# The head of each MLP: pinned norm matmuls, earlier first weights, three square buffers, and k outermost

## The chip, the cores and the metric

The kernel runs on one core of a Trainium2 chip. Its engines are TensorE (PE: matmuls and, listed apart as PEld, its weight loads), VectorE (DVE), ScalarE (ACT), GpSimd (POOL) and SyncE (SP, which here only issues DMAs). Each takes its own instructions in the order written; semaphores tie them together. The metric is the device time of one execution in microseconds.

## The reference

A two-layer bidirectional encoder is applied to a prompt of 256 and a sample of 512 tokens with shared weights (model width 1024, 64 per head, MLP width 4096). Cut to what matters here:

```python
for layer in range(2):
    h = rmsnorm(x, ln_mix[layer])
    x = x + attention(h) @ w_out          # layer 0: neighbourhood + grouped-query, layer 1: differential
    h = rmsnorm(x, ln_mlp[layer])         # x * rsqrt(mean(x*x) + 1e-6) * g
    x = x + square(relu(h @ w_up[layer])) @ w_down[layer]
return rmsnorm(x, ln_f)
```

All is float32.

## The kernel before

**Layout.** The 512 and 256 tokens are laid side by side, so x is eight tiles x[0] to x[7] of 128 features by 768 tokens. Every float32 operand of a large matmul is split in two fp32r parts, `hi` (a rounded copy, by ACT) and `lo` (the rest, by DVE), and a product is three matmuls: hi x hi, hi x lo, lo x hi. For weights this is `wsplit` (L77 to L82), with tiles wraw (three buffers, loaded through SP at L75), whi and wlo (four buffers each, `whilo`, L90).

**The head** is `out_proj_norm` (L753) with `up_plain` (L823). The output projection's last two of eight k tiles are applied here, in two token halves of 384 (`EVEN`), since they depend on the last attention heads. For each half: eight products of six matmuls (opc, L778), each added to x[m] by DVE (L780), squared by ACT (L144) and summed into acc (L149), the second to fifth tile's by POOL, the sixth's and seventh's by DVE; the last square stays apart in `parts`. `rstd` (L152) multiplies acc and that last square with ones on TensorE (ss, L158), DVE scales (ms, L161), POOL takes the power -1/2 (rt, L163); `spread` (L166) brings rt to all partitions on TensorE (pb, L177) and DVE copies it to R (L179). Then for each of the eight k, DVE forms xn = x * g * R (L763), ACT its hi part xh (L766) and DVE its lo part xl (L767).

The square's buffer has the tag `sq`, one buffer of 768 columns. xn, `up_plain`'s av and the sums' t share the tag `st`, three buffers of 384 columns.

**The up projection** comes in groups of four blocks (f) of 128 hidden features. In group 0, `up_plain`: for each half, for each f, for each k, three matmuls (upc, L837); then Relu, Square and the hi part hh by ACT (L839 to L842) and the lo part hl by DVE (L843). f 0 and 1 use the first pair of weight tiles, f 2 and 3 the second. The other groups use `up_fast` (L849), a Strassen-like scheme that needs sums of the xn parts: T (three sets of four pairs) and t4. `sums` (L797) forms them after `up_plain`: for each of four kk it recomputes two n = x * g * R over all 768 tokens (L763; tag `av`, three buffers), then t1, t2, t3 and t4 (L805 to L813), with their splits.

**The down projection** of a group (`down`, L922) makes eight output tiles, two at a time, each in two PSUM tiles (dna, dnb, L202), and DVE adds them to x (L932). Group 0's is called with `cover`, which takes the first two of four k for both of the first two tiles ahead of the others. It runs after `sums` in the order written. The last group of layer 1 has `final` (L936), which does the down projection, the sum of squares, the last norm (L964) and the stores for 512 tokens and then for 256; its matmuls are fin (L953).

PSUM has eight banks: three for the tag `mm`, five for `at` (L33).

**What sets the order.** A planner orders each engine's instructions ahead of time: it simulates the program with its own costs, takes of the ready instructions the one written first, and gives out buffers as it goes. Reads and writes of the same tile keep their written order, so a DVE add to x[k] comes after the sums' reading of x[k]. Nothing else fixes where `rstd` and `spread` stand among TensorE's products.

## Time and profile before

| what | value |
|---|---|
| median of 3 runs | 1855.36 us (1855.0 to 1857.76) |
| the profiled execution | 1855.08 us, of which the span of the profile is 1853.3 us |
| mean granted clock of TensorE | 0.986 |
| PE busy, PEld busy | 97%, 92% |
| DVE, ACT, POOL busy | 61%, 45%, 14% |
| layer 0's head, first opc to first dna | 350.88 to 423.56 us |
| layer 1's head, first opc to first dna | 1278.72 to 1354.77 us |

In the rows of the timeline, the first two numbers are start and length in us, then engine, line, operation, `out<-in` by the program's tile names, shapes, and in brackets the engine's idle time before it with what ended it. A row of waits reads "engine tile line <- engine tile line waited for: total us, times, longest". A row of stretches has bounds, length, each engine's busy time with its instructions, TensorE's granted clock, the DMA engines' busy share and GB/s. A row of groups ends with busy us, mean ns of one, and idle us before them.

### The profile page before, as it was taken

The numbers are of one execution on the slowest core, as the hardware profiler recorded it, in microseconds if no ns is written. First come the engines' busy times: TensorE is split into PE (matmuls) and PEld (weight loads), VectorE is DVE, ScalarE is ACT, GpSimd is POOL, SyncE is SP. The second block draws the span as 40 slices with busy tenths as digits, with TensorE's granted clock in tenths as the row PEclk, the third lists the DMA queues.
The fourth block names the chain that finished last, engine by engine and source line by source line (L and its number), as shares of the span: only waits on it lengthen the run. The fifth ranks groups of instructions, "written<-read, shape, count | busy, mean of one in ns | idle before, by whom it ended". The sixth has DMA issues, their size and how long they took to land.

```text
span 1853.3 us, 28804 instructions
## 1 busy us (share of the span) xinstructions
PE 1796.7 (97%) x11382; PEld 1710.5 (92%) x11382; DVE 1123.6 (61%) x2238; ACT 828.7 (45%) x1733; POOL 259.4 (14%) x340
## 2 busy tenths in 40 slices
PE   7999999989999999999999999999899999999997
PEld 7878888889999999999999999987899999999996
DVE  8877555568645544554566676775685455455545
ACT  6765443344533433343435555554445334334434
POOL 4411000110100100010221221211101001000003
PEclk9999999989999999999999999999799999999998
DMA  5111224102523433343410111122025334333432
GB/s 171 47 32 38 72 64 162 52 23 69 134 60 96 114 88 78 95 110 88 133 53 25 45 47 38 35 93 65 24 57 131 75 97 110 85 81 91 114 86 80
DMA packets 52328, 146.33 MB, mean 79 GB/s; under 512 B 6113, under 2 KB 8929, under 8 KB 52193
## 3 DMA queue, kind: packets, MB, share of 16 engines
q1 hardware_dynamic: 38080, 119.82, 20.5%
q0 software_dynamic: 12096, 22.03, 7.6%
q10 hardware_dynamic: 2016, 2.64, 0.4%
q8 instruction: 90, 1.47, 0.3%
q14 instruction: 46, 0.37, 0.1%
HBM read 137.38 MB, written 6.29 MB: 78 GB/s over the span
## 4 chain that ended last, share of the span: by engine, by line
PE 88%; DVE 6%; ACT 3%; POOL 2%; issue 1%; DMA 1%; DVEq 0%; SPq 0%; ACTq 0%; POOLq 0%
PE dna L202 13%; PE dnb L202 13%; PE upx L882 13%; PE dqk L189 8%; PE upz L882 6%; PE dvp L189 4%; PE opa L202 4%; PE upy L882 3%; PE upc L837 3%; PE npa L202 2%; PE ds L268 2%; PE dpv L711 2%; PE opb L202 2%; PE fin L953 2%; PE qp L189 1%; PE vp L189 1%
## 5 line engine op out<-in xcount | busy, mean ns | idle before, releaser
L81 ACT ACTIVATE whi<-wraw 128x1024 fp32r<-128x1024 f32 (+2 forms) x168 | 171.7, 1023 | 194.7 <-PE dnb L202 92.6
L82 DVE TENSOR_TENSOR wlo<-wraw,whi 128x1024 fp32r<-128x1024 f32 (+2 forms) x172 | 201.9, 1180 | 88.8 <-ACT whi L81 87.9
L88 POOL DMA_DIRECT2D wlo<-in_w_up_dram x84 | 74.0, 881 | 847.7 <-ACT wlo L87 462.1
L932 DVE TENSOR_TENSOR x<-dna,x 128x384 f32<-128x384 f32 x120 | 66.7, 556 | 177.1 <-PE dna L202 177.1
L202 PE MATMUL dna<-hh,whi 128*128 128x384 f32 x480 | 162.8, 339 | 3.7 <-DVE x L932 3.7
L202 PE MATMUL dnb<-hh,whi 128*128 128x384 f32 x480 | 162.6, 339 | 0.4 <-DVE x L932 0.4
L202 PE MATMUL dna<-hh,wlo 128*128 128x384 f32 x480 | 162.7, 339 | 0.0
L202 PE MATMUL dna<-hl,whi 128*128 128x384 f32 x480 | 162.4, 338 | 0.0
L202 PE MATMUL dnb<-hh,wlo 128*128 128x384 f32 x480 | 162.4, 338 | 0.0
L202 PE MATMUL dnb<-hl,whi 128*128 128x384 f32 x480 | 162.3, 338 | 0.0
L86 ACT ACTIVATE whi<-wraw 128x512 fp32r<-128x512 f32 x84 | 52.7, 628 | 185.7 <-PE dnb L202 152.6
L189 PE MATMUL dqk<-whi,xh 128*128 128x256 f32 x384 | 115.6, 301 | 0.0
L882 PE MATMUL upx<-T,whi 128*128 128x384 f32 x448 | 115.2, 338 | 0.0
L189 PE MATMUL dqk<-whi,xl 128*128 128x256 f32 x384 | 108.5, 283 | 0.0
L189 PE MATMUL dqk<-wlo,xh 128*128 128x256 f32 x384 | 108.5, 282 | 0.0
L202 PEld LDWEIGHTS dna<-hh,whi 128*128 128x128 f32 x480 | 90.5, 188 | 4.4 <-DVE x L932 4.4
L696 ACT ACTIVATE de<-ds,m 128x512 f32<-128x512 f32 (+1 forms) x96 | 58.4, 613 | 80.4 <-DVE m L694 80.2
L202 PEld LDWEIGHTS dnb<-hh,whi 128*128 128x128 f32 x480 | 90.4, 188 | 0.8 <-DVE x L932 0.8
L202 PEld LDWEIGHTS dna<-hl,whi 128*128 128x128 f32 x480 | 90.5, 188 | 0.0
L202 PEld LDWEIGHTS dna<-hh,wlo 128*128 128x128 f32 x480 | 90.4, 188 | 0.0
L202 PEld LDWEIGHTS dnb<-hl,whi 128*128 128x128 f32 x480 | 90.3, 188 | 0.0
L202 PEld LDWEIGHTS dnb<-hh,wlo 128*128 128x128 f32 x480 | 90.3, 188 | 0.0
(271 smaller groups left out, 5164.4 us busy)
## 6 DMA issues: line engine op xcount, KB each, us to landing
wraw<-in_w_down_dram SPq DMA_DIRECT2D x68, 512.0 KB, 3.9
wraw<-in_w_up_dram SPq DMA_DIRECT2D x64, 512.0 KB, 3.6
wlo<-in_w_up_dram POOLq DMA_DIRECT2D x84, 256.0 KB, 4.9
wraw<-in_w_in_o_dram SPq DMA_DIRECT2D x24, 512.0 KB, 3.6
wraw<-in_w_in_e_dram SPq DMA_DIRECT2D x16, 512.0 KB, 3.7
x<-in_xT_dram SPq DMA_DIRECT2D x16, 384.0 KB, 5.6
nbias<-in_bias_dram SPq DMA_DIRECT2D x20, 256.0 KB, 3.7
wraw<-in_w_out_e_dram SPq DMA_DIRECT2D x8, 384.0 KB, 3.0
```

The source lines that it names most:

```text
L81: nc.scalar.activation(hi, raw, AF.Copy)
L82: nc.vector.tensor_tensor(out=lo, in0=raw, in1=hi.bitcast(F32), op=ALU.subtract)
L86: nc.scalar.activation(hi, raw, AF.Copy)
L88: nc.gpsimd.dma_start(lo, src, accum_op=ALU.add)
L189: nc.tensor.matmul(ps[:, :256], st[:, tk], col(k, part, 0, 256), start=(k == 0 and i == 0), stop=(k == KD - 1 and i == 2))
L202: nc.tensor.matmul(ps[:, : e - s], lhs(k, part), mv[:, s:e], start=(k == 0 and i == 0), stop=(k == nk - 1 and i == 2))
L268: nc.tensor.matmul(out[h], q(a_, hp, qs), k(b_, hp, ks), start=i == 0, stop=i == 2)
L696: nc.scalar.activation(e, s, AF.Exp, bias=m, scale=1.0, accum_out=l2[:, c : c + 1])
L711: nc.tensor.matmul(pv, pt[:, i * P : (i + 1) * P], v[:, k0 // P + i, vc], start=(i == 0), stop=(i == nk - 1))
L837: nc.tensor.matmul(ps, lhs(k, part), mv[:, s:e], start=(n == 0 and j == 0), stop=(n == KD - 1 and j == 2))
L882: nc.tensor.matmul(ps, w[part][:, c], mv, start=(start and kk == 0 and j == 0), stop=(stop and kk == KH - 1 and j == 2), skip_group_check= ...
L932: evac_halves(*ps[mi], lambda p, s: nc.vector.tensor_tensor(out=xm[:, s], in0=p, in1=xm[:, s], op=ALU.add), EVEN)
```

## The change

It has five parts.

1. *Places of the norm matmuls.* `issue_after(i)` binds the instructions traced in its block that run on the engine of i to come after i there. `woven` cuts other products in three pieces: after the first come `rstd`'s matmuls, after the second `spread`'s, then the third. For the first half the pieces are the second half's output products 0 to 2, 3 to 5, and 6 and 7. For the second half they are the up products of the first half: all 48 matmuls of blocks 0 and 1, 24 of blocks 2 and 3, the other 24.
2. *First weights.* The first pair of w_up tiles is loaded and split (`up_ws`) in the text right after the output projection's two tiles, ahead of all products of the head, and passed on.
3. *Square buffers.* The head's squares take the tag `st` with three buffers of 384 columns. `Norm` keeps the start column of each part with it; `final` and the norm ahead of layer 1 keep their one `sq` buffer.
4. *k outermost.* In `up_plain` two blocks go together, one in an `mm` bank, one in an `at` bank: for each k, three matmuls for the one and three for the other, so both end together.
5. *Priorities and banks.* `sums` is traced with its priority lowered by 500 (`LATER`). `final` takes the two PSUM tiles of a pair from `mm` and `at` instead of both from `mm`.

```diff
+LATER = 500
...
     def add(self, x, last=KD):
...
-                sq = self.temp()
-                nc.scalar.activation(sq[:, s], x[:, s], AF.Square)
+                sq = self.temp()[:, : s.stop - s.start]
+                nc.scalar.activation(sq, x[:, s], AF.Square)
...
     def rstd(self):
...
+                    self.last = nc.tensor.matmul(ss[:, 2 * i : 2 * i + 2], part[:, t * P - s0 : (t + 1) * P - s0], ones,
+                                                 start=j == 0, stop=j == len(self.parts) - 1)
...
     def out_proj_norm(src, o, x, g, mp):
         os_ = [split(o[k], "o") for k in (6, 7)]
         ws = [wtile(src, 1024) for _ in range(2)]
+        up_ws = [[wtile("w_up", 1024) for _ in range(2)]]
...
+        norms = [Norm(lambda: mp.tile([P, NH], F32, tag="st", name="sq", bufs=3), half, acc) for half in EVEN]
+        def product(i, m):
+            sl = slice(*EVEN[i])
+            ps = ps_tile(("mm", "at")[m % 2], "opc")[:, :NH]
+            hi, lo = ws[m // 4]
+            for k in range(2):
+                for j, (part, mv) in enumerate(((0, os_[k][0]), (0, os_[k][1]), (1, os_[k][0]))):
+                    c = ((m % 4) * 2 + k) * P
+                    last = nc.tensor.matmul(ps, (hi, lo)[part][:, c : c + P], mv[:, sl],
+                                            start=(k == 0 and j == 0), stop=(k == 1 and j == 2))
+            nc.vector.tensor_tensor(out=x[m][:, sl], in0=ps, in1=x[m][:, sl], op=ALU.add)
+            norms[i].add(x[m], KD - 1)
+            return last
...
-        for i, (s, e) in enumerate(EVEN):
-            sl = slice(s, e)
-            nm = Norm(lambda: mp.tile([P, NT], F32, tag="sq", name="sq", bufs=1), (s, e), acc)
-            for m in range(KD):
...
-            nm.spread(nm.rstd(), R)
+        def split_half(i):
+            sl = slice(*EVEN[i])
             for k in KORD:
...
+        def woven(i, work):
+            nm, last = norms[i], None
+            for step, piece in enumerate(work):
+                with tc.issue_after(last.ins) if last else nullcontext():
+                    last = piece()
+                with tc.issue_after(last.ins):
+                    if step == 0:
+                        rt = nm.rstd()
+                    elif step == 1:
+                        nm.spread(rt, R)
+                        split_half(i)
+                last = nm.last
+        products = lambda i, ms: lambda: [product(i, m) for m in ms][-1]
+        products(0, range(KD))()
+        woven(0, [products(1, ms) for ms in (range(3), range(3, 6), range(6, 8))])
...
-    def up_plain(xs, mp):
-        ws = [[wtile("w_up", 1024) for _ in range(2)] for _ in range(GF // 2)]
+    def up_plain(xs, mp, ws, second_half):
+        ws.append([wtile("w_up", 1024) for _ in range(2)])
...
+        def pair(i, f0):
+            s, e = EVEN[i]
+            pss = [ps_tile(t, "upc")[:, :NH] for t in ("mm", "at")]
+            for n, k in enumerate(KORD):
+                for f, ps in enumerate(pss):
                     for j, (part, mv) in enumerate(((0, xs[k][0]), (0, xs[k][1]), (1, xs[k][0]))):
+                        last = nc.tensor.matmul(ps, lhs(f0 + f, k, part), mv[:, s:e],
+                                                start=(n == 0 and j == 0), stop=(n == KD - 1 and j == 2))
+                if n % 2 and n < KD - 1:
+                    yield last
...
+            yield last
+        first = joined.from_iterable(pair(0, f0) for f0 in range(0, GF, 2))
+        take = lambda n: lambda: [next(first) for _ in range(n)][-1]
+        second_half([take(4), take(2), take(2)])
+        for f0 in range(0, GF, 2):
+            run(pair(1, f0))
         return hs
...
     def final(hs, x, sq):
...
-                ps = [ps_tile("mm", "fin")[:, : e - s] for _ in range(2)]
+                ps = [ps_tile(t, "fin")[:, : e - s] for t in ("mm", "at")]
...
     def mlp(layer, x, state, mp):
-        hs = up_plain(xs, mp)
-        sums()
+        hs = up_plain(xs, mp, up_ws, second_half)
+        with tc.high_priority(offset=-LATER):
+            sums()
         down(hs, x, True)
```

More of the change, by code (lines that the diff above doesn't have):

```diff
@@ L1 @@
 import math
-from contextlib import ExitStack
+from contextlib import ExitStack, nullcontext
+from itertools import chain as joined
 import numpy as np
@@ L135, in __init__ @@
             self.acc = cpool.tile([P, NT], F32, tag="acc", name="acc", bufs=1) if acc is None else acc
-            self.parts = [self.acc]
+            self.parts = [(self.acc, 0)]
         def add(self, x, last=KD):
@@ L142, in add @@
             else:
-                sq = self.temp()
-                nc.scalar.activation(sq[:, s], x[:, s], AF.Square)
+                sq = self.temp()[:, : s.stop - s.start]
+                nc.scalar.activation(sq, x[:, s], AF.Square)
                 if self.n == last:
-                    self.parts.append(sq)
+                    self.parts.append((sq, s.start))
                 else:
                     eng = nc.vector if self.n >= 5 else nc.gpsimd
-                    eng.tensor_tensor(out=self.acc[:, s], in0=self.acc[:, s], in1=sq[:, s], op=ALU.add)
+                    eng.tensor_tensor(out=self.acc[:, s], in0=self.acc[:, s], in1=sq, op=ALU.add)
             self.n += 1
@@ L156, in rstd @@
             for i, t in enumerate(self.tiles):
-                for j, part in enumerate(self.parts):
-                    nc.tensor.matmul(ss[:, 2 * i : 2 * i + 2], part[:, t * P : (t + 1) * P], ones,
-                                     start=j == 0, stop=j == len(self.parts) - 1)
+                for j, (part, s0) in enumerate(self.parts):
+                    self.last = nc.tensor.matmul(ss[:, 2 * i : 2 * i + 2], part[:, t * P - s0 : (t + 1) * P - s0], ones,
+                                                 start=j == 0, stop=j == len(self.parts) - 1)
             ms = spool.tile([P, TT], F32, tag="ms", name="ms", bufs=2)[:, :n]
@@ L176, in spread @@
                     i = self.tiles.index(t)
-                    nc.tensor.matmul(pb[:, t * P - s : t * P - s + P], rt[:, i : i + 1].broadcast_to([P, P]), ident,
-                                     start=True, stop=True)
+                    self.last = nc.tensor.matmul(pb[:, t * P - s : t * P - s + P], rt[:, i : i + 1].broadcast_to([P, P]), ident,
+                                                 start=True, stop=True)
                 nc.vector.tensor_copy(R[:, s:e], pb[:, : e - s])
@@ L757, in out_proj_norm @@
         ws = [wtile(src, 1024) for _ in range(2)]
+        up_ws = [[wtile("w_up", 1024) for _ in range(2)]]
         acc = cpool.tile([P, NT], F32, tag="acc", name="acc", bufs=1)
         R = cpool.tile([P, NT], F32, tag="R", name="R", bufs=1)
-        xs = []
+        xs = [None] * KD
+        norms = [Norm(lambda: mp.tile([P, NH], F32, tag="st", name="sq", bufs=3), half, acc) for half in EVEN]
[11 more added lines that the diff above has]
+            return last
         def normed(k, out, s):
@@ L767, in parts @@
             nc.vector.tensor_tensor(out=lo, in0=src, in1=hi.bitcast(F32), op=ALU.subtract)
-        for i, (s, e) in enumerate(EVEN):
-            sl = slice(s, e)
-            nm = Norm(lambda: mp.tile([P, NT], F32, tag="sq", name="sq", bufs=1), (s, e), acc)
-            for m in range(KD):
-                ps = ps_tile(("mm", "at")[m % 2], "opc")[:, :NH]
-                hi, lo = ws[m // 4]
-                for k in range(2):
-                    for j, (part, mv) in enumerate(((0, os_[k][0]), (0, os_[k][1]), (1, os_[k][0]))):
-                        c = ((m % 4) * 2 + k) * P
-                        nc.tensor.matmul(ps, (hi, lo)[part][:, c : c + P], mv[:, sl],
-                                         start=(k == 0 and j == 0), stop=(k == 1 and j == 2))
-                nc.vector.tensor_tensor(out=x[m][:, sl], in0=ps, in1=x[m][:, sl], op=ALU.add)
-                nm.add(x[m], KD - 1)
-            nm.spread(nm.rstd(), R)
+        def split_half(i):
+            sl = slice(*EVEN[i])
             for k in KORD:
                 if i == 0:
-                    while len(xs) < KD:
-                        xs.append(None)
                     xs[k] = [xpool.tile([P, NT], F32R, tag=t, name=t, bufs=8) for t in ("xh", "xl")]
@@ L818, in last_sum, with lhs @@
                 parts(xs[kk][0][:, b], xs[kk][1][:, b], t4s[kk])
-        return xs, T, sums, last_sum
-    def up_plain(xs, mp):
-        av = []
-        ws = [[wtile("w_up", 1024) for _ in range(2)] for _ in range(GF // 2)]
+        return xs, T, lambda work: woven(1, work), sums, last_sum, up_ws
+    def up_plain(xs, mp, ws, second_half):
+        ws.append([wtile("w_up", 1024) for _ in range(2)])
         hs = [htiles(mp) for _ in range(GF)]
-        for i, (s, e) in enumerate(EVEN):
-            for f in range(GF):
-                def lhs(k, part):
-                    c = 512 if k < KH else 0
-                    hi_lo = ws[f // 2][(f % 2 == 0) != (k < KH)]
-                    return hi_lo[part][:, c + (k % KH) * P : c + (k % KH) * P + P]
-                ps = ps_tile(("mm", "at")[f % 2], "upc")[:, :NH]
-                for n, k in enumerate(KORD):
-                    for j, (part, mv) in enumerate(((0, xs[k][0]), (0, xs[k][1]), (1, xs[k][0]))):
-                        nc.tensor.matmul(ps, lhs(k, part), mv[:, s:e], start=(n == 0 and j == 0), stop=(n == KD - 1 and j == 2))
+        def lhs(f, k, part):
+            c = (512 if k < KH else 0) + (k % KH) * P
+            return ws[f // 2][(f % 2 == 0) != (k < KH)][part][:, c : c + P]
+        def pair(i, f0):
[3 more added lines that the diff above has]
+                for f, ps in enumerate(pss):
+                    for j, (part, mv) in enumerate(((0, xs[k][0]), (0, xs[k][1]), (1, xs[k][0]))):
+                        last = nc.tensor.matmul(ps, lhs(f0 + f, k, part), mv[:, s:e],
+                                                start=(n == 0 and j == 0), stop=(n == KD - 1 and j == 2))
+                if n % 2 and n < KD - 1:
+                    yield last
+            for f, ps in enumerate(pss):
                 av = mp.tile([P, NH], F32, tag="st", name="av", bufs=3)
@@ L840, in up_plain @@
                 nc.scalar.activation(av, av, AF.Square)
-                hh, hl = hs[f]
+                hh, hl = hs[f0 + f]
                 nc.scalar.activation(hh[:, s:e], av, AF.Copy)
                 nc.vector.tensor_tensor(out=hl[:, s:e], in0=av, in1=hh[:, s:e].bitcast(F32), op=ALU.subtract)
+            yield last
[4 more added lines that the diff above has]
+            run(pair(1, f0))
         return hs
@@ L967, in mlp @@
     def mlp(layer, x, state, mp):
-        xs, T, sums, last_sum = state
-        hs = up_plain(xs, mp)
-        sums()
+        xs, T, second_half, sums, last_sum, up_ws = state
+        hs = up_plain(xs, mp, up_ws, second_half)
+        with tc.high_priority(offset=-LATER):
+            sums()
         down(hs, x, True)
```

## The prediction

> **What bounds the kernel now.** I read the page first, then TensorE's waits in the two stretches between the last attention matmuls and the first down projection (the "heads"), then the granted clock there, then each waiting matmul's neighbours on the timeline.

> ```profile
> span 1853.3 us, 28804 instructions
> PE 1796.7 (97%) x11382; PEld 1710.5 (92%) x11382; DVE 1123.6 (61%) x2238; ACT 828.7 (45%) x1733; POOL 259.4 (14%) x340
> ```

> TensorE is the bound, so only its idle time (56.6 us in all) and its slow time can be won. The waits of layer 0's head and first down projection (from 340 to 465 us), then of layer 1's (1270 to 1400); the columns are total, count, longest:

> ```profile
> PE ss L158 <- DVE acc L149: 7.4, 2, 4.5
> PE dna L202 <- DVE x L932: 1.9, 1, 1.9
> PE upc L837 <- DVE wlo L82: 1.8, 2, 1.5
> PE upc L837 <- ACT xh L766: 0.4, 1, 0.4
> PE upc L837 <- DVE xl L767: 0.3, 1, 0.3
> ```

> ```profile
> PE ss L158 <- DVE acc L149: 6.0, 2, 3.4
> ...
> PE upc L837 <- DVE wlo L82: 1.4, 1, 1.4
> PE pb L177 <- POOL rt L163: 0.7, 1, 0.7
> PE dnb L202 <- DVE x L932: 0.4, 1, 0.4
> ```

> The norm's matmuls wait most, for the sum of squares. The stretches below show what follows such waits; the columns are bounds, length, busy time of PE, its weight loads, DVE, ACT and POOL with their instructions, granted clock, DMA share, GB/s:

> ```profile
> 368.50:371.90 3.40, 3.40 (x14) 3.38 (x14) 1.16 (x3) 0.00 (x0) 0.86 (x1) 0.50 0.00 0
> 389.00:399.20 10.20, 8.34 (x31) 7.87 (x32) 3.06 (x7) 1.63 (x4) 0.86 (x1) 0.50 0.00 0
> 443.60:447.00 3.40, 3.40 (x13) 3.40 (x12) 3.40 (x8) 0.84 (x2) 0.00 (x0) 0.50 0.00 0
> 1296.90:1303.80 6.90, 6.23 (x26) 5.83 (x25) 2.75 (x6) 0.82 (x2) 0.87 (x1) 0.51 0.01 2
> 1314.00:1317.40 3.40, 3.40 (x11) 2.94 (x11) 0.86 (x1) 0.53 (x1) 2.73 (x2) 0.50 0.75 217
> 1320.80:1331.10 10.30, 9.63 (x35) 9.15 (x36) 3.74 (x8) 2.09 (x4) 0.87 (x1) 0.50 0.00 0
> ```

> TensorE works there at half clock. Work that takes t at 0.50 would take t/2: the heads' five stretches (all but the third) lose (3.40+8.34+6.23+3.40+9.63)/2 = 15.5 us, the down projection's 1.7.

> **The square chain.** Why is the sum late? Layer 0's first product and its first half, then its second half, others left out:

> ```profile
> 350.88 0.42 PE L778 MATMUL opc<-oh,whi 128*128 128x384 f32 x1
> 358.05 1.03 POOL L149 TENSOR_TENSOR acc<-acc,sq 128x384 f32<-128x384 f32 x1 [170.53 <-ACT sq L144]
> 359.72 1.02 POOL L149 TENSOR_TENSOR acc<-acc,sq 128x384 f32<-128x384 f32 x1 [0.64 <-ACT sq L144]
> 363.02 1.00 POOL L149 TENSOR_TENSOR acc<-acc,sq 128x384 f32<-128x384 f32 x1 [0.64 <-ACT sq L144]
> 364.61 0.56 DVE L149 TENSOR_TENSOR acc<-acc,sq 128x384 f32<-128x384 f32 x1 [3.20 <-ACT sq L144]
> 366.46 0.35 PE L158 MATMUL ss<-ones,acc 128*128 128x2 f32 x2 [2.87 <-DVE acc L149]
> 381.91 2.35 DVE L82 TENSOR_TENSOR wlo<-wraw,whi 128x1024 fp32r<-128x1024 f32 x2
> 382.56 2.57 POOL L149 TENSOR_TENSOR acc<-acc,sq 128x384 f32<-128x384 f32 x1 [0.63 <-ACT sq L144]
> 390.83 0.56 PE L158 MATMUL ss<-ones,acc 128*128 128x2 f32 x2 [4.52 <-DVE acc L149]
> ```

> With one square buffer ACT squares only after POOL has added: one tile takes 359.72-358.05 = 1.67 us instead of POOL's 1.02.

> **The change, part by part.**

> *Three buffers, first half.* Four POOL adds back to back end at 358.05+4x1.02 = 362.1. The hand-over to DVE takes 364.61-364.02 = 0.6, two DVE adds about 1.1, the hand-over to PE 0.1: the matmul could start at 363.95. PE is free at 366.46-2.87 = 363.6, so 0.4 stays (0 to 1.3, if the last squares lack a buffer). The place of this norm matmul is not new: TensorE stops there 12.7 us after its first product, which is room for the 66 products (at 0.173, below) after which the diff pins it, and some attention work between. Layer 1's first wait is its 6.0 less 3.4 = 2.6. Both halves of that: -2.9-2.6+0.8 = **-4.7 us**.

> *Second half.* The squares follow their products from about 364 on, instead of from about 380 (their second add is the 382.56 row), since they no longer wait for the one buffer that the first half's last square holds. The matmul is pinned behind 48 up products (8.3 us). PE reaches the first spread at 363.95+1.3 (an estimate for the norm's matmuls, the last of which takes 0.36 below)+3.1 = 368.4 and, with 0.7 for the spread and 12 products more, the up products at 371.2, so the pinned place at 379.5. On DVE R is copied from 369.2, and the first half's split (8 times 0.61 and 0.55, below, less overlap: about 8.6) ends near 378; the last square's add follows. So chain and PE arrive together. I leave 0.5 in each layer (0 to 3): -4.5-3.4+1.0 = **-6.9 us**. The three buffers are the ones of xn; a square that holds one slows the split, which the k-pace below contains. PE keeps its order, so whatever a pinned matmul waits, all later products wait, and ACT's Relu and DVE's hl behind them.

> *rt.* From the last matmul of the sum to the spread, by way of ms on DVE and rt on POOL, 1.8 us pass:

> ```profile
> 368.10 0.36 PE L158 MATMUL ss<-ones,sq 128*128 128x2 f32 x2
> 369.94 1.48 PE L177 MATMUL pb<-ident,rt 128*128 128x128 f32 x6
> 461.19 2.08 PE upx L882 x12
> ```

> The last row, from the chain of waits, gives a product's price at full clock, 2.08/12 = 0.173. Eighteen of them (3.1 us) will stand between; one more POOL add (1.02) ahead of rt still fits. Layer 1's 0.7 goes: **-0.7** (0 to -0.7).

> *First weights ahead.* Nothing: the second tile of the first pair is split here, ahead of the first product at 350.88 already.

> ```profile
> 350.37 1.06 ACT L81 ACTIVATE whi<-wraw 128x1024 fp32r<-128x1024 f32 x1 [2.55 <-PE opb L202]
> ```

> The late pair (381.91 above) is the second, which needs the buffers of the output projection's weights and stays behind the split on DVE. SP's loads and their order stay too. If tracing them early put a wlo (2.35/2 above) in front of the o split on DVE, 1.2 us would be late once a layer; I take 0.

> *k outermost.* Two products use each k, so PE wants a new k every 6 x 0.173 = 1.04 us rather than 0.52. DVE makes one in about 1.07 (rows below, spaced closer than their length). The k-waits (0.4+0.3) and weight waits (1.8+1.4) make 3.9; the pace and the second pair's wlo still cost an estimated 1.0 per layer (0 to 3): **-1.9 us**. Both tiles of a pair now end together, so the last hh/hl come about 4 us after the last product; the down projection's first 24 products (4.2 us) cover that, and uncovered it would cost up to 2.

> *Clock.* 15.5 us if no wait is left; I keep one slow stretch of 3.4 us (1.7) for the waits that I left: **-13.8** (-15.5 to -7). [...]

> *Sums later.* Their work, from the second R to the last T (397.4 to 444.8), and what follows until T is read:

> ```profile
> 397.40:444.80 47.40, 45.53 (x253) 45.22 (x253) 38.75 (x67) 29.12 (x56) 1.96 (x2) 0.97 0.22 56
> 444.80:465.00 20.20, 20.20 (x111) 20.20 (x110) 14.76 (x27) 3.72 (x6) 0.87 (x1) 0.95 0.17 49
> 410.00:426.00 16.00, 16.00 (x94) 16.00 (x93) 7.50 (x11) 10.01 (x18) 0.00 (x0) 1.00 0.21 67
> L763 DVE SCALAR_TENSOR_TENSOR n<-x,gains,R 128x768 f32<-128x768 f32 x8 | 8.0, 1009 | 0.0
> L763 DVE SCALAR_TENSOR_TENSOR xn<-x,gains,R 128x384 f32<-128x384 f32 x8 | 4.5, 611 | 0.0
> L767 DVE TENSOR_TENSOR xl<-xn,xh 128x384 fp32r<-128x384 f32 x8 | 4.0, 549 | 0.0
> 441.88 0.55 DVE L932 TENSOR_TENSOR x<-dna,x 128x384 f32<-128x384 f32 x1
> ```

> x's first add stood at 441.88 behind the sums, and PE waited 1.9 for its PSUM bank. Now the adds go first, but x[k] may only be added to after the sums have read it (n<-x), and n has three buffers: PE's fourth tile pair, 25 us into the projection, still needs nearly all sums done. DVE has 38.8+14.8 = 53.5 us of work between R and the use of T (fourth figure of the stretches). PE's own way there becomes 24 products, then 96, then 192, then 24: 336 x 0.173 = 58 us. So 4.5 us are free. All of 1.9+1.9+0.4+1.7 = 5.9 could go; I take half, **-3** (-5.9 to +10, second rival).

> *Final.*

> ```profile
> 1829.25 6.34 DVE L964 TENSOR_TENSOR x<-x,R 128x512 f32<-128x512 f32 x5
> 1835.98 0.42 PE L953 MATMUL fin<-hh,whi 128*128 128x256 f32 x1 [3.66 <-DVE x L957]
> ```

> Taking PSUM from two tags frees PE from this 3.66 us, but the adds still stand behind DVE's 6.34, and then the square chain, still with one buffer here, paces the end. I take **-0.8** (0 to -3.7).

> Sum: -4.7-6.9-0.7-1.9-13.8-3-0.8 = -31.8. The profiled execution took 1855.08, 1.8 above its span and 0.3 below the median of the runs: **1823 us**.

> **Rivals.**

> 1. *POOL is shut out.* The 382.56 add took 2.57 beside DVE's wlo instead of 1.02: 1.55 more for 1.7 us side by side, so POOL all but stood. If the second half's last two POOL adds fall under the first half's split on DVE, which also reads two SBUF tiles, they end 2 us after it; with hand-over and DVE adds the sum is there at 378+2+0.6+1.1 = 381.7 or later, and PE waits 2 to 3 us more and runs two slow stretches (3.4): 6 per layer, **1835**. For it: that row. Against: products 3 to 5 end before R, so their squares can be first. [...]
> 2. *Sums too late.* If DVE's 8.5 idle us between 410 and 426 stay, its way to T is 62 us against 58: 4 us of waiting, a slow stretch (1.7) and the 1.5 of gain per layer lost: 7.2 twice, **1837**. For it: 53.5 of 58. Against: T had 20 us to spare.
> 3. *Slower: the down projection of group 0 runs in turns with the sums.* If nothing of them fills DVE's gaps earlier, x's adds (L932) wait for reads that stand last in DVE's queue, and PE for the banks. The sums are 8.0+4.4+5x2.2 = 23 us (the quoted n row, the T rows' 8 x 0.55 and five times 4 x 0.55, a length that L932 shows too), each of four groups leaving a slow stretch (1.7): 30 per layer, 1823+2x30 = **1883**. It decides from about 16 us per layer on. Against: DVE takes whatever is ready, and has nothing else.
> 4. *It does not do what it says.* xn, av and t take the three buffers so that squares still get one; the norm matmuls sit where they sat: **1854**.

> **How the numbers follow.** Forecast 0.58, rivals 0.15, 0.15, 0.07, 0.05. A measurement of this kernel tells 0.2% (3.7 us) from no change: faster 0.58+0.15+0.15 = 0.88, same 0.05, slower 0.07. The forecast's own range is 1812 (every wait and slow stretch named gone: 2.9+2.6+7.9+0.7+3.9+15.5+5.9+3.7 = 43) to 1832 (half of the upper ends of four terms beyond what I took: first sums 2x0.9, second 2x2.5, pace 2x2, clock 6.8). Rivals 1 and 2 lie at 1835 and 1837, and with half of those ends beside them near 1843; what lies above is 3 and 4. So 1812 to 1843.

> **What will show it.** Right: the wait of ss for acc falls from 13.4 us in the heads to about 2; POOL's L149 adds follow each other at about 1.0; one slow stretch or none per head; first dna about 72.6-14 us after the first opc; L932 adds ahead of the sums. Wrong: 2 us POOL adds beside L763 and L767 and a wait of ss above 2 (rival 1); upx or upz waiting for T (2); dna waiting for L932 above 5 (3); squares 1.65 apart (4).

## The result

The changed kernel took 1828.70 us (median of four runs, 1826.64 to 1831.16) against 1855.75 us (1855.00 to 1857.76) for the kernel before in the same comparison: a ratio of 0.9853, 95% interval 0.9836 to 0.987. The forecast was 1823, its range 1812 to 1843. Measured a second time, beside the experiments below, the changed kernel took 1823.53 us (1822.53 to 1824.61) against 1858.39 (1855.07 to 1861.64): 0.9814 (0.98 to 0.9828). Executions of one kernel differ by some us here, and the section on the runs shows by what.

### The profile page after: what moved, and what is told of

It reads as the page before. It is cut to its first block, busy times and chain, and to the rows that moved or that the text cites. A ratio compares the mean times of both kernels' runs of the same rounds, so it can differ in the third digit from the quotient of the medians.

```text
span 1824.8 us, 28828 instructions
## 1 busy us (share of the span) xinstructions
PE 1783.9 (98%) x11382; PEld 1702.1 (93%) x11382; DVE 1122.2 (61%) x2238; ACT 827.3 (45%) x1733; POOL 259.3 (14%) x340
## 4 chain that ended last, share of the span: by engine, by line
PE 90%; DVE 5%; ACT 2%; issue 1%; POOL 1%; DMA 0%; DVEq 0%; ACTq 0%; POOLq 0%
PE dna L204 14%; PE dnb L204 14%; PE upx L917 13%; PE dqk L191 8%; PE upz L917 6%; PE dvp L191 4%; PE upc L861 4%; PE opa L204 4%; PE upy L917 3%; PE npa L204 2%; PE ds L270 2%; PE dpv L713 2%; PE opb L204 2%; PE qp L191 1%; PE vp L191 1%
## 5 line engine op out<-in xcount | busy, mean ns | idle before, releaser
L967 DVE TENSOR_TENSOR x<-dna,x 128x384 f32<-128x384 f32 x120 | 66.8, 557 | 172.9 <-PE dna L204 172.6
```

Source lines behind the costliest of these rows:

```text
L967: evac_halves(*ps[mi], lambda p, s: nc.vector.tensor_tensor(out=xm[:, s], in0=p, in1=xm[:, s], op=ALU.add), EVEN)
```

## The profile after, against the profile before

The first profiled execution of the changed kernel took 1826.64 us, its span is 1824.8 us. Its stages are read from where certain products start. In the timeline of the changed kernel, layer 0's first opc, dna and upx and the first fin (layer 1's are read in the same way):

```profile
352.31 0.42 PE L774 MATMUL opc<-oh,whi 128*128 128x384 f32 x1
412.96 0.34 PE L204 MATMUL dna<-hh,whi 128*128 128x384 f32 x1
446.76 0.34 PE L917 MATMUL upx<-xh,whi 128*128 128x384 f32 x1
1769.09 0.40 PE L988 MATMUL fin<-hh,whi 128*128 128x512 f32 x1
```

The differences of such starts, with those of the kernel before and of the second profile of the changed kernel (span 1822.2), in us:

| stage | before | changed | changed, second profile |
|---|---|---|---|
| start to first opc | 350.88 | 352.31 | 352.18 |
| layer 0's head, opc to dna | 72.68 | 60.65 | 60.63 |
| layer 0's first down projection, dna to upx | 37.47 | 33.80 | 33.80 |
| from there to layer 1's opc | 817.69 | 817.10 | 817.67 |
| layer 1's head | 76.05 | 63.39 | 60.94 |
| layer 1's first down projection | 36.58 | 33.80 | 33.80 |
| from there to the first fin | 408.05 | 408.04 | 408.04 |
| first fin to the end of the span | 53.90 | 55.71 | 55.14 |

In the first profile the heads gave 24.7 us and the down projections 6.45; the last stretch cost 1.8, the start 1.4 and the rest gave 0.6: 28.5 together, the difference of the spans (1853.3 - 1824.8). The start isn't the change's: up to the first opc the instructions stand in the same order on every engine as before, and in the profiles of the kernels below that stretch took anything from 350.7 to 355.0.

TensorE's waits in the changed kernel, in layer 0's head and down projection (345 to 450 us), layer 1's (1260 to 1362) and the last stretch (1765 to 1825); total, count, longest:

```profile
PE upc L861 <- ACT xh L784: 1.8, 1, 1.8
PE upc L861 <- DVE xl L785: 0.8, 1, 0.8
```

```profile
PE upc L861 <- ACT xh L784: 1.9, 1, 1.9
...
PE upc L861 <- DVE xl L785: 0.7, 1, 0.7
PE ss L160 <- DVE acc L151: 0.4, 1, 0.4
```

```profile
PE ss L160 <- DVE acc L151: 6.9, 1, 6.9
```

The 13.4 us for which the heads' norm matmuls waited are 0.4; nothing waits for wlo, nor dna for the x adds (L967 now). What remains in the heads is that 0.4 and one start-up wait per layer for the first xh and xl. In the last stretch a wait of 6.9 us stands where 3.7 us for a PSUM bank stood.

The heads' stretches at half clock, in the form of the prediction's rows (the granted clock is the third figure from the right):

```profile
377.00:380.50 3.50, 3.50 (x13) 3.50 (x12) 3.50 (x8) 1.92 (x4) 0.00 (x0) 0.51 0.00 0
1288.40:1295.30 6.90, 6.19 (x20) 5.80 (x19) 6.90 (x16) 3.81 (x8) 0.00 (x0) 0.51 0.00 0
```

By the same working as before (half of PE's busy time) the heads now lose (3.50+6.19)/2 = 4.8 us instead of 15.5. Halving is a little high: in the first of these stretches a product follows the other after 0.32 us (from 377.33 to 380.21), where 0.173 is the price at full clock.

**The start-up wait, row by row.** From the timeline of layer 0's head, POOL's and DVE's rows around the first spread, and the two waits of TensorE:

```profile
359.48 4.30 POOL L151 TENSOR_TENSOR acc<-acc,sq 128x384 f32<-128x384 f32 x4 [170.57 <-ACT sq L146]
368.74 2.96 POOL L151 TENSOR_TENSOR acc<-acc,sq 128x384 f32<-128x384 f32 x2
369.15 1.69 DVE L84 TENSOR_TENSOR wlo<-wraw,whi 128x1024 fp32r<-128x1024 f32 x1 [0.36 <-ACT whi L83]
370.76 1.01 DVE L776 TENSOR_TENSOR x<-opc,x 128x384 f32<-128x384 f32 x2
371.69 0.54 DVE L181 COPY R<-pb 128x384 f32<-128x384 f32 x1
373.11 0.56 DVE L151 TENSOR_TENSOR acc<-acc,sq 128x384 f32<-128x384 f32 x1 [0.88 <-POOL acc L151]
373.59 1.67 DVE L781 SCALAR_TENSOR_TENSOR xn<-x,gains,R 128x384 f32<-128x384 f32 x3
374.81 0.62 PE L861 MATMUL upc<-xh,whi 128*128 128x384 f32 x2 [1.76 <-ACT xh L784]
376.24 0.44 PE L861 MATMUL upc<-xl,whi 128*128 128x384 f32 x1 [0.82 <-DVE xl L785]
```

The first half's four POOL adds follow each other at 4.30/4 = 1.08, and ss needs no wait. Then two POOL adds fall beside a wlo: 2.96 for the two (1.01 for one alone, at 366.94), and 1.69 for the wlo (1.22 where POOL rests, 388.21 in a row below). R is copied behind that wlo and two x adds, and DVE then stands 0.88 at an add that waits for POOL, ahead of the first xn.

## The experiments

A ratio is that of a kernel to the kernel before on the same chip; the kernels were spread over three chips, and the changed kernel's 0.9814 is from one of them. A difference of 0.001 is 1.9 us, and the intervals reach about 0.0015 to either side. But the changed kernel itself had 0.9853 in the first comparison, 0.0039 (7 us) more, so smaller differences than that are read here from the stages of the profiles, and not from the times.

**The changed kernel again** (no edit).

> The changed kernel itself once more, beside the others. The four kernels that differ from it in one detail each (banks, places, order of k, sixth add) all came out at 1822.6 to 1823.9, 5 us under its 1828.7, although their heads wait nearly as long. If the details are what they gain (1.8 to 2 us each by their waits), it is at 1826 to 1829 again, 3 to 5 above them; if most of it is how the granted clock falls in one execution or another, it comes out at 1824 to 1826, and its first profile was an unlucky one: the first opc near 351 instead of 352.3, layer 1's head at 61 instead of 63.4 us.

1823.53 us, 0.9814 (0.98 to 0.9828), the lower case. Layer 1's head took 60.94 us, 2.45 less than in the first profile, with the same instructions; the first opc, expected near 351, came at 352.18. TensorE's waits in layer 1's head, from the timeline, and a stretch:

```profile
1279.06 0.38 PE L160 MATMUL ss<-ones,acc 128*128 128x2 f32 x2 [0.48 <-DVE acc L151]
1289.51 0.61 PE L861 MATMUL upc<-xh,whi 128*128 128x384 f32 x2 [1.38 <-ACT xh L784]
```

```profile
1281.40:1284.80 3.40, 3.40 (x13) 3.40 (x13) 2.68 (x3) 1.47 (x2) 3.32 (x4) 0.53 0.02 5
```

Here the half clock came once, behind ss with its wait of 0.48, and not after the upc wait; in the first profile it came for 6.9 us after the upc wait and not behind ss. Each of these stretches is about 3.4 us or a multiple. So the same work costs one slow stretch, about 1.7 us, more or less per head from one execution to the next. The runs' mean granted clock goes with it: 0.993 to 0.995 here, 0.988 to 0.992 in the first comparison.

What places the stretches the traces do show. In steps of 0.1 us, all 44 of them that end before their kernel does, in the heads, the down projections and the last products of the thirteen traces, start and end on a grid of 3.413 us that runs through the whole execution: within one trace they agree with it to 0.01 us, and from trace to trace it lies elsewhere (a stretch starts at 368.47 in the kernel before, at 377.07 and 377.06 in the two profiles of the changed one, at 375.77 with both tiles from mm). Take the windows of this grid, from about 275 us on, that are at full clock and hold no ss: all 35 in which PE was busy for 1.60 us or less are followed by one at half clock, none of 5670 with 1.83 or more is, and of five between three are. So in these traces TensorE is at half clock behind a window in which it works for about half of the 3.413 us or less (the change lies between 1.60 and 1.83), and a wait is dear or free by where the grid cuts it; the run with f outermost, below, shows a wait with both prices.

**One square buffer.**

```diff
-        norms = [Norm(lambda: mp.tile([P, NH], F32, tag="st", name="sq", bufs=3), half, acc) for half in EVEN]
+        norms = [Norm(lambda: mp.tile([P, NT], F32, tag="sq", name="sq", bufs=1), half, acc) for half in EVEN]
```

> The changed kernel, but the head's squares go through one buffer again. My theory (chain: the single buffer makes the sum late, and TensorE slows down behind each wait): each tile of the chain takes 1.67 us again instead of 1.02, so the first ss wait returns at about 2.5 to 3 us in each layer, and the second half's squares start only when the first half's last square has been read by ss; 8 to 15 us more than the changed kernel's 1828.7, so 1837 to 1844. Rival (places: the gain is in where the norm matmuls stand in TensorE's queue, and not in the buffers): within 3 us of the changed kernel, 1826 to 1832.

1834.98 us, 0.9872 (0.9855 to 0.9888): 0.0058 above the changed kernel, 10.8 us. The heads took 65.54 and 67.09 us. Rows of layer 0's timeline, and a stretch:

```profile
359.40 1.02 POOL L151 TENSOR_TENSOR acc<-acc,sq 128x384 f32<-128x384 f32 x1 [170.49 <-ACT sq L146]
361.05 1.02 POOL L151 TENSOR_TENSOR acc<-acc,sq 128x384 f32<-128x384 f32 x1 [0.63 <-ACT sq L146]
367.73 0.59 PE L160 MATMUL ss<-ones,acc 128*128 128x2 f32 x2 [2.44 <-DVE acc L151]
390.74 0.28 PE L160 MATMUL ss<-ones,acc 128*128 128x2 f32 x2
367.60:374.50 6.90, 6.77 (x25) 6.72 (x26) 2.71 (x6) 2.52 (x4) 2.35 (x3) 0.51 0.00 0
```

The adds are 1.65 apart again, the first half's ss waits 2.44 (2.9 in layer 1), and 6.9 us at half clock follow in each layer. By the profiles the heads are 8.6 and 11.1 us longer than in the two of the changed kernel. But the second half's ss, at 390.74, waits for nothing even so. The chain theory holds for the first half alone.

**Three square buffers alone**, in the kernel before.

```diff
-            nm = Norm(lambda: mp.tile([P, NT], F32, tag="sq", name="sq", bufs=1), (s, e), acc)
+            nm = Norm(lambda: mp.tile([P, NH], F32, tag="st", name="sq", bufs=3), (s, e), acc)
```

> The kernel before, with the head's squares in the three buffers of xn and nothing else. If the buffers alone carry the head's gain: the ss waits fall from 13.4 us in the heads to about 2 or 3, the heads gain 15 to 20 us, 1836 to 1840. If the order of TensorE's queue is needed too (the planner puts the first ss behind 55 products here instead of 66, and the second one 11 products after the spread instead of 48): ss waits of 2 us or more stay in front of each half with slow stretches behind, and the gain is under 10 us: 1846 or more.

1846.74 us, 0.9943 (0.9929 to 0.9956): 10.5 us of the 34.9 that the whole change gives. The heads took 70.16 and 70.45. In the timeline of layer 0, the first ss and the rows around the second half:

```profile
368.10 0.56 PE L158 MATMUL ss<-ones,acc 128*128 128x2 f32 x2 [2.00 <-DVE acc L149]
382.09 1.50 DVE L767 TENSOR_TENSOR xl<-xn,xh 128x384 fp32r<-128x384 f32 x3 [0.37 <-ACT xh L766]
382.79 0.93 ACT L144 ACTIVATE sq<-x 128x384 f32<-128x384 f32 x2
383.50 2.41 DVE L780 TENSOR_TENSOR x<-opc,x 128x384 f32<-128x384 f32 x5
387.74 0.56 DVE L149 TENSOR_TENSOR acc<-acc,sq 128x384 f32<-128x384 f32 x1 [1.82 <-POOL acc L149]
388.21 1.22 DVE L82 TENSOR_TENSOR wlo<-wraw,whi 128x1024 fp32r<-128x1024 f32 x1
389.48 0.69 PE L837 MATMUL upc<-xh,wlo 128*128 128x384 f32 x1 [4.25 <-DVE wlo L82]
```

In both layers the first ss still waits 2.0 us. Three buffers alone let the planner put it behind 55 and 57 matmuls of the output projection; in the changed kernel it stands behind 66, and the sum is there in time or 0.4 late. In the second half five of the x adds stand on DVE behind the first half's split (382.09, then 383.50), though their products, made from 373.61 on, were all done by 380.7; so the squares come at 382.79, the sum at 388, and the second pair's wlo behind it. TensorE now waits 4.25 us for that wlo instead of 4.52 for ss: the lateness has another name. In the changed kernel the order in which the program is written puts six of the second half's products, with their adds and squares, ahead of the first half's split, and DVE does those adds before R (370.76 above).

**No pins.**

```diff
-                with tc.issue_after(last.ins) if last else nullcontext():
+                with nullcontext():
                     last = piece()
-                with tc.issue_after(last.ins):
+                with nullcontext():
```

> The changed kernel, with the norm's matmuls left to the planner instead of pinned behind a given product. My theory: with three square buffers the planner puts them at almost the same places (66 products of the first half ahead of ss, as with the pins; the second half's ss one product later), so the time is within 2 us of 1828.7. Rival (places): without the pins ss comes early again and waits, 10 us or more above the changed kernel, 1839 or more.

1823.45 us, 0.9819 (0.9803 to 0.9835): no difference from the changed kernel. The pins carry nothing that shows: without them the first ss stands behind the same 66 matmuls and the second behind 49 up matmuls instead of 48. Its layer 0 shows again that a wait doesn't fix its price:

```profile
374.55 0.80 PE L861 MATMUL upc<-xh,whi 128*128 128x384 f32 x3 [1.75 <-ACT xh L784]
375.99 0.44 PE L861 MATMUL upc<-xl,whi 128*128 128x384 f32 x1 [0.64 <-DVE xl L785]
```

Nearly the waits of the changed kernel, a granted clock of 1.00 throughout, and a head of 58.92 instead of 60.65.

**f outermost again in group 0.**

```diff
-            for n, k in enumerate(KORD):
-                for f, ps in enumerate(pss):
+            for f, ps in enumerate(pss):
+                for n, k in enumerate(KORD):
```

(with the points at which the norm's pieces are woven in moved to the fourth k and the end of each tile)

> The changed kernel, but group 0's up products run through all k for one tile and then for the next, as before (pairs of weights and pins are kept). My theory: TensorE asks for a new k every 0.52 us while VectorE makes one per 1.07 us, so the first up tile waits up to 8 x 0.55 = 4.4 us for the split of k, less what it has been given ahead, and runs a slow stretch behind it: 2 to 5 us more per layer, so 1833 to 1839. Rival (the wait after R is one start-up delay that no order of k changes): the same 2.5 us of waits and 1828.7 within 2.

1823.89 us, 0.9823 (0.9808 to 0.9837): the rival. The waits are those of the changed kernel:

```profile
373.33 0.61 PE L861 MATMUL upc<-xh,whi 128*128 128x384 f32 x2 [1.76 <-ACT xh L784]
374.77 0.44 PE L861 MATMUL upc<-xl,whi 128*128 128x384 f32 x1 [0.83 <-DVE xl L785]
```

k outermost gains nothing that can be measured: after these two waits TensorE waits for no k, whichever loop is outside. The price of the waits differs, though, by the grid: in the changed kernel they leave PE 1.44 us of work in one window, and the half clock of 377.07 follows (first row); here they leave 1.83, and the next window is at full clock (the two others).

```profile
373.65:377.07 3.42, 1.44 (x7) 1.12 (x8) 3.42 (x9) 1.89 (x4) 0.00 (x0) 1.00 0.02 6
```

```profile
372.57:375.99 3.42, 1.83 (x9) 1.52 (x10) 3.42 (x8) 1.57 (x3) 0.00 (x0) 1.00 0.00 0
375.99:379.40 3.41, 3.41 (x22) 3.41 (x21) 3.41 (x8) 2.30 (x5) 0.00 (x0) 1.00 0.00 0
```

**Sums first, in the changed kernel; and sums later alone, in the kernel before.**

```diff
-LATER = 500
+LATER = 0
```

```diff
-        sums()
+        with tc.high_priority(offset=-500):
+            sums()
```

> The changed kernel, but the first sums are not put later (LATER = 0), so they come before the x adds of the down projection in DVE's order as before. My theory: the wait of dna for x (1.9 and 0.4 us in the kernel before) and the slow stretch behind it are back; down takes about 6 us more over the two layers (37.5 and 36.6 us from first dna to first upx instead of 33.8 twice), so about 1835. Rival (the down projection gained because the head before it left DVE less work behind): the down projection keeps its 33.8 us, and the time stays within 2 us of 1828.7.

> The kernel before with the first sums put 500 later and nothing else. If the delay is enough for itself: the waits of dna and dnb for x (1.9 and 0.4 us) go, the down projections fall from 37.5 and 36.6 to 33.8 us, 6.4 less in all, 1849 to 1851 against 1855.8 to 1857.5. If it is the shorter head that made room: T comes late in front of upx (rival 2), or dna still waits, and less than 3 us are gained, 1853 or more.

The first took 1836.40 us, 0.9885 (0.987 to 0.9901), 13.2 us above the changed kernel; its down projections took 39.74 and 38.74 us. In layer 0, the wait in the timeline and the stretch around it:

```profile
433.31 0.69 PE L204 MATMUL dna<-hh,whi 128*128 128x384 f32 x1 [3.18 <-DVE x L967]
432.20:439.00 6.80, 5.69 (x18) 5.69 (x19) 6.65 (x15) 2.04 (x4) 0.00 (x0) 0.51 0.00 1
```

The second took 1848.45 us, 0.9948 (0.9935 to 0.9961): the down projections are 33.80 us each, and the heads 74.28 and 74.77, together as long as in the kernel before. So the delay works by itself: 6.45 us by the profiles, 9.9 by the medians. In the changed kernel it is worth more, 10.9 us of down projection by the profiles; there the head brings TensorE to layer 0's first dna 12.0 us sooner after the first opc than before, while the first x add of the kernel with the sums first comes 10.7 us sooner, so that the wait grows from 1.9 to 3.2.

**The last stretch: banks, buffers, order.** With both PSUM tiles from mm again; with that and three buffers for the last squares; and with the first segment's scaling and stores two tiles at a time behind the second segment's x adds, those stores all through SyncE (two tags, three buffers, the sixth add on GpSimd):

```diff
-                ps = [ps_tile(t, "fin")[:, : e - s] for t in ("mm", "at")]
+                ps = [ps_tile("mm", "fin")[:, : e - s] for _ in range(2)]
```

```diff
-        sq = lambda: mp.tile([P, NT], F32, tag="sq", name="sq", bufs=1)
+        sq = lambda: mp.tile([P, NT], F32, tag="av", name="sq", bufs=3)
```

```diff
+                for _ in range(2):
+                    if later:
+                        later.pop(0)()
             nm.spread(nm.rstd(), R)
-            for k in range(KD):
+            def out(k, sl=sl, queues=(nc.sync, nc.scalar if s else nc.sync)):
...
+            later = [lambda k=k, out=out: out(k) for k in range(KD)]
```

> The changed kernel, but the last products take both PSUM tiles from the tag mm, as before. My theory: the stretch from the first fin to the end, which grew from 53.9 to 55.7 us, goes back to 53.9, since the order planned for ACT puts the last segment's squares ahead of the stores again; 1827 (1.8 less). Rival (the growth comes from the phase of the clock windows at the end and not from the banks): it stays at 55.7 and 1828.7.

> The changed kernel; in the last stretch the squares have three buffers and both PSUM tiles come from mm again. My theory: the square chain of one buffer (1.25 us per tile) paces the last segment's sum, and TensorE stands 6.9 us for it and does the spread at half clock; with three buffers ScalarE can square ahead, the wait falls to 2 to 4 us: first fin to the end 49 to 52 us, 1823 to 1826. Rival (the x adds on VectorE pace it, not the buffer): 53 to 54 us, 1827.

> The changed kernel with the sixth add of the second half on GpSimd, three buffers for the last squares, and the scaling and storing of the first segment's output written two tiles at a time behind the x adds of the second segment's products, those stores on SyncE's queue alone. My theory: the last stretch loses time because the x adds stand behind VectorE's five scalings (6.34 us), whichever banks are used; with the adds first, TensorE stands neither 3.7 us for a bank nor 6.9 us for ss, and the stretch from the first fin to the end falls from 53.8 (55.7 with two tags) to 49 to 51 us; with about 0.5 us per layer from the sixth add 1818 to 1822. Rival: the stores of the first segment, now later, pile up in front of the second segment's (1 MB more to land at the end), and the stretch stays at 53 to 55 us.

The first took 1822.81 us (0.9814, 0.9799 to 0.983), first fin to the end 53.82; the second 1822.59 (0.9817, 0.9802 to 0.9832), 53.59; the third 1819.66 (0.9793, 0.9779 to 0.9807), 52.80. The times of the first two don't differ from the changed kernel's 0.9814; the stretch does, and why two tags cost 1.3 to 1.9 us in it is in the changed kernel's timeline:

```profile
1795.79 0.41 DVE L992 TENSOR_TENSOR x<-fin,x 128x256 f32<-128x256 f32 x1
1800.83 5.37 ACTq L1000 DMA_DIRECT2D out_dram<-x  x4
1806.24 0.42 ACT L146 ACTIVATE sq<-x 128x256 f32<-128x256 f32 x1 [10.36 <-DVE x L992]
1807.49 0.42 ACT L146 ACTIVATE sq<-x 128x256 f32<-128x256 f32 x1 [0.29 <-POOL acc L151]
1816.04 1.23 PE L179 MATMUL pb<-ident,rt 128*128 128x128 f32 x4 [1.04 <-POOL rt L165]
```

The planned order has ScalarE issue four stores ahead of the last segment's second square. That square's x add was done at 1796.2, ten microseconds before it; what it stood behind is the stores, the last of them issued at 1806.2, and not the add that its bracket names. From there the one square buffer goes by POOL's adds, 1.25 us a tile. TensorE, done early, stands idle and is at half clock for ss and the spread (the four spread matmuls 1.23, against 0.71 with mm, below). With both tiles from mm the old wait for the bank is back, and the end is sooner:

```profile
1801.98 0.39 PE L988 MATMUL fin<-hh,whi 128*128 128x256 f32 x1 [3.69 <-DVE x L992]
1811.00 0.71 PE L179 MATMUL pb<-ident,rt 128*128 128x128 f32 x4 [1.04 <-POOL rt L165]
```

In this order the second square stands ahead of the stores. Three buffers with these banks change little (rival): the x adds behind DVE's scalings pace the sum. In the third kernel TensorE waits for no bank; its sum:

```profile
1800.06 3.93 POOL L151 TENSOR_TENSOR acc<-acc,sq 128x256 f32<-128x256 f32 x4
1805.90 0.55 PE L160 MATMUL ss<-ones,acc 128*128 128x2 f32 x2 [3.73 <-DVE acc L151]
```

I had expected 49 to 51 us for the stretch and got 52.8: POOL's part of the scalings ends at 1800.06, and its four adds pace the sum (DVE's add behind them waits 1.89 for them). Still this stretch is the shortest, and the time is the lowest: its five runs (1819.64 to 1819.78) lie below all four of the changed kernel's on the same chip.

**The second half's sixth add on GpSimd.**

```diff
-                    eng = nc.vector if self.n >= 5 else nc.gpsimd
+                    eng = nc.vector if self.n >= (6 if self.seg.start == NH else 5) else nc.gpsimd
```

> The changed kernel, with the sixth add of the second half's sum on GpSimd instead of VectorE. My theory for the head's last wait: VectorE stands blocked 0.88 us by that add, which it reaches before GpSimd's fifth is done, ahead of the first xn; without it the first up product comes 0.9 us sooner per layer, waits 2.0 instead of 2.8 us: 1826.5. Rival (the wait is set by the R copy and the split after it, whatever stands between, or the longer GpSimd chain makes the second ss wait by 1 us): no change or up to 2 us more, 1828.7 to 1831.

1823.83 us, 0.9818 (0.9805 to 0.9832), no difference, though the start-up waits are a little shorter (1.03 and 1.10 in layer 0 instead of 1.76 and 0.82). Half a microsecond per layer is below what these runs tell apart. DVE's block of 0.88 is gone, but POOL's fifth add and the moved sixth now run beside the first xn, and three of those take 2.95 us instead of 1.67:

```profile
374.64 2.95 DVE L781 SCALAR_TENSOR_TENSOR xn<-x,gains,R 128x384 f32<-128x384 f32 x3
```

## Why the prediction was right, step by step

- **Three buffers, first half (-4.7).** Right in size, and in half of the cause: 2.9 and 2.6 us of waiting are 0 and 0.4, POOL's adds are 1.08 apart, and with one buffer 2.44 and 2.9 come back. But with three buffers alone 2.0 stay in each layer, since ss then moves ahead to 55 and 57 matmuls. The step took its place (64 and 68 before) as given; in the changed kernel it stands, with or without pins, at 66, behind the three products of the second half that the text puts ahead of it.
- **Second half (-6.9).** Right in size, wrong in cause. Its waits (4.5 and 3.4) are gone. But the step said that the squares come earlier "since they no longer wait for the one buffer", and that isn't what held them: with three buffers alone they still start at 382.79, and with one buffer in the changed kernel ss doesn't wait. What held them was DVE's place for the second half's x adds, behind the first half's split. What is left to have freed them, with the pins, the buffers and the loop order excluded one by one, is the order in which the woven products are written, which the step took only for TensorE's places. That order was not run by itself, so this cause is argued and not shown.
- **rt (-0.7).** Right: pb waits only in the last stretch.
- **First weights ahead (0).** Right as far as the traces show: up to the first opc every engine has its instructions in the same order as before. It was not run by itself.
- **k outermost (-1.9).** Wrong. The wlo waits went (1.8 and 1.4), but they stay away with f outermost too. The waits for k were priced as a pace, 1.0 per layer; they are a start-up, from R's copy to the first xh and xl, of about 2.6 us per layer in both loop orders (1.4 in layer 1 of the second profile). So the five waits of 3.9 us became four of 5.2 in the first profile and three of 4.0 in the second: +1.3 and +0.1 where -1.9 stood.
- **Clock (-13.8).** Right that the slow stretches go with the waits, size a little off: 15.5 - 4.8 = 10.7 in the first profile; in the second (3.50+3.40)/2 = 3.5 are left, so 12.0. I had kept one slow stretch for both heads together; there are two or three. The 2.87 us of waiting ahead of the first slow stretch of before are no bound: the quoted stretch at 443.60 stood behind a wait of 1.9 already, 0.48 us with ss behind it did it too, and 1.75 and 0.64 in a row didn't. It isn't the length of the wait that decides in these traces, but how much work is left in a window of the grid (1.60 us or less, against 1.83 or more).
- **Sums later (-3).** Right in kind, half the size: 6.45, all of the 5.9 and a little more. I took half because DVE's work of 53.5 us had to fit in TensorE's 58. The rows of the changed kernel for the same way, from R to T, bear both out, and it just fits:

```profile
392.30:446.80 54.50, 54.50 (x313) 54.50 (x313) 48.18 (x83) 26.48 (x50) 2.00 (x2) 1.00 0.22 59
446.80:451.10 4.30, 4.30 (x26) 4.30 (x25) 4.13 (x8) 2.55 (x6) 0.87 (x1) 1.00 0.43 125
419.64 0.56 DVE L967 TENSOR_TENSOR x<-dna,x 128x384 f32<-128x384 f32 x1
451.59 0.55 DVE L834 SCALAR_TENSOR_TENSOR T<-t,T 128x384 fp32r<-128x384 f32 x1
452.50 0.52 PE L917 MATMUL upx<-T,whi 128*128 128x384 f32 x2
```

DVE was busy 48.2+4.1 = 52.3 of 58.8 us; the first x add comes at 419.64 instead of 441.88; the last write of T ends at 451.59+0.55 = 452.1, and TensorE reads on through T at 452.50 with no wait.
- **Final (-0.8).** Wrong in sign: +1.8 in the first profile and +1.2 in the second. The step saw that the adds stand behind the 6.34 and that the square chain paces the end; it didn't look at where ScalarE's queue has the stores, nor at the half clock at which TensorE, idle for 6.9 us, then does ss and the spread (1.23 us instead of 0.71).

The heads' terms as measured in the first profile, -13.0 (ss), -0.7, +1.3 and -10.7, make -23.1 of the 24.7 that the heads gave; in the second, -12.9, -0.7, +0.1 and -12.0 make -25.5 of 27.2. The other 1.6 or 1.7 are put down to nothing. The sum was -31.8; the spans of the two profiles give -28.5 and -31.1. That the second measurement lies at 1823.5 is partly luck: in its profile 2.0 too little from the k step, 1.8 from the clock, 2.0 from the final and 1.3 lost at the start are set off by 3.5 more from the sums, 1.3 more from ss and the 1.7 of no known source.

**The rivals.** POOL shut out: its wait didn't come (the second ss doesn't wait, since POOL's adds are over before the split), but longer operations side by side are there in small, at the late pair's wlo (two POOL adds 2.96, where one alone takes 1.01) and beside the first xn once the sixth add goes to POOL. They feed the start-up wait. Here DVE's own operations are longer too (the wlo 1.69 instead of 1.22, the three xn 2.95 instead of 1.67). That the two SBUF tiles which the split reads would do it was my estimate; what does it is not shown. Sums too late: no wait for T. Down in turns with the sums: no wait for L967; at LATER = 0 it waits once per layer, 3.2 us, far from the 30 of that rival. It doesn't do what it says: not so for the squares, which get their buffers (1.08 apart), and 1854 is far off. But the pins and k outermost gain nothing that was measured, and the first weights moved nothing up to the first opc; the gain goes with the three square buffers and the late sums, as the runs show, and by exclusion with the written order.

## What to carry to other kernels

Before crediting a buffer or a pin, read on the engine that feeds the chain what stands ahead of the late instruction: here the second half's adds stood on DVE behind the first half's split, and the order in which the program is written is what is left to explain most of what neither the buffers alone (10.5 us) nor the late sums alone (9.9) gave of 34.9. Where TensorE's clock falls after short waits (here 0.48 us with ss behind it), price a wait with a range (nothing to two slow stretches), and compare kernels by several runs: single profiles of the same kernel differed by 2.5 us in one head, and its medians by 5 us. And a wait taken from an engine near the end may only move: follow the chain through every queue, stores included, to the last instruction.
